# First query block of the scores: one product against both parts of the keys, the low half added through the mask

## Chip, cores and metric

The kernel runs on one core of one Trainium2 chip. The metric is the device time of one execution in microseconds (us). The kernel before was timed three times; the median is 364.83 us (364.63 to 365.72). The engines are named as the profile names them: PE is TensorE's matrix products, PEld its weight loads, DVE is VectorE, ACT is ScalarE, POOL is GpSimd, SP is SyncE, which here issues the transfers.

## What is computed

One decoder layer over 256 tokens of width 1024, all in float32. For this case the attention matters:

```python
proj = x @ w_in[l]
q, k, v = ...                       # 8 heads of 64
q = apply_partial_rope(q, cos, sin); k = apply_partial_rope(k, cos, sin)
s = einsum("hqd,htd->hqt", q, k) * scale
s = where(key_pos <= q_pos, s, -inf)
p = softmax(s, axis=-1)
y_att = einsum("hqt,htd->hqd", p, v) @ w_attn_out[l]
```

There is one block of 256 keys, so the block selection of the reference selects nothing and every query sees the keys up to its own position. Beside attention run a short gated convolution, two gates, a normalisation, and a feed-forward part of width 2816 with a second normalisation.

## The kernel before, in words

Every float32 operand of a product is split in a high part h and a low part l = x - h. A product is then made of three: h·h + h·l + l·h, summed in PSUM. For the weights ACT writes the high part (`split_h`, L196) and DVE the low part (`split_l`, L205), one unit of 128 x 1024 at a time, from a buffer `raw` that SP fills (three buffers; a transfer is issued once its buffer is free).

From the end of q, k and v on, the program goes through the units of the weights in order, `slot` by `slot` (L496). C0 is the first unit of the convolution's input h. A slot first issues the products of its unit on PE, then the ACT and PE steps that the table `beside` holds for it, then `split_h` for the unit five ahead, then `split_l` for the unit four ahead, then the DVE steps. `at` (L486) appends a step to a slot, `at_once` (L489) puts it in front of the others of its kind in that slot. Nothing else orders the work: each engine runs its instructions in the order in which they were issued, and waits at an instruction whose data or buffer isn't ready.

Two kinds of PSUM banks are used in this stage, four of each, taken in rotation. Those named acc hold the products of the units: a pair of units gets its high products by `cols_wide` (L333, 512 columns) and its low ones by `cols_narrow` (L340, 256 columns). In order of time they are h0, c0, b0, h1, c1, b1, then the gates g. So c10 and c11 (the two units of c1) take the banks of b00 and b01. A bank comes free when ACT has copied its upper half out (`conv_sum_act`, L620) and DVE has added its lower half to that (`conv_sum_dve`, L624). Those named ps hold the scores, the transposes and the results of attention.

Attention is done for four pairs of heads p = 0 to 3. `qk_transpose`, `qk_h` and `qk_l` leave in `qkT[head rows, part, group, token]` the transposed queries (groups 0 to 3) and keys (groups 4 to 7), part 0 being high and part 1 low. A pair has two heads j in the two halves of the 128 rows, so a product of the scores uses 64 rows. Then:

- `scores` (L392, product at L402) runs twice, for p = 0, 1 in slot C0+4 and for p = 2, 3 in slot C0+9. For each pair and head it has one bank: columns 0 to 127 for the first block of 128 queries (t = 0, which needs only 128 keys), columns 256 to 511 for the second (t = 1, 256 keys). Each of these is three products, and the two heads' products stand next to each other. One call is 24 products, of which 12 have 128 columns (t = 0) and 12 have 256 (t = 1).
- `masked` (L405, DVE at L412) adds the mask to the scores, scales them and finds the maximum, in one instruction per block and head, t = 0 first; L415 negates the maxima. It stands in slots C0+5, C0+7, C0+10 and C0+12.
- `exps` (L418, ACT at L423) follows one slot after each, `normalize` (L427) and `probs_T` (L435) later, then `attend`.

Of the kernel before, what the change touches and what calls it, by code (L numbers as in the profile page):

```python
# [12 lines left out]
AF = mybir.ActivationFunctionType  # L13
ALU = mybir.AluOpType

P = 128
# [11 lines left out]
SCALE = 1.0 / math.sqrt(HD)  # L28
# [109 lines left out]
def layer_kernel(ctx: ExitStack, tc: tile.TileContext, x, wpack, cpack, ln1_g, ln1_b, ln2_g, ln2_b, out):  # L138
    nc = tc.nc
# [13 lines left out]
    def ps_bank(name):  # L153
        return ps_pool.tile([P, 512], F32, tag="ps", name=name)

    def scratch(shape, name, bufs=None, tag="scr"):
        return tmp.tile(shape, F32, tag=tag, name=name, bufs=bufs or 6)
# [93 lines left out]
    MASK = [mask[:, 0:128], mask[:, 128:384]]  # L251
    PCOL = [slice(0, 128), slice(128, 384)]
# [100 lines left out]
    qkT = big.tile([P, 2, KT, S], F32R, tag="b16", name="qkT")  # L353
# [36 lines left out]
    SB, SM, PR = {}, {}, {}  # L390

    def scores(ps):  # L392

        for p in ps:
            SB[p] = [ps_bank(f"s{p}_{j}") for j in range(2)]
        for t in range(2):
            n = (t + 1) * P
            for p in ps:
                for a, b in ((0, 0), (0, 1), (1, 0)):
                    for j in range(2):  # L400
                        hs = slice(j * HD, (j + 1) * HD)
                        nc.tensor.matmul(SB[p][j][:, t * 256:t * 256 + n], qkT[hs, a, p, t * P:(t + 1) * P],  # L402
                                         qkT[hs, b, 4 + p, 0:n], start=a + b == 0, stop=a == 1)

    def masked(p):  # L405
        st = tmp.tile([P, 16], F32, tag="st", name=f"st{p}", bufs=4)
        if p == 2:
            SM["late"] = big.tile([P, 2, 2, 384], F32, tag="rows", name="sm23")
        sm = scratch([P, 2, 384], f"sm{p}", tag="pr", bufs=2) if p < 2 else SM["late"][:, p - 2]
        for t in range(2):  # L410
            for j in range(2):
                nc.vector.tensor_tensor_reduce(  # L412
                    out=sm[:, j, PCOL[t]], in0=SB[p][j][:, t * 256:t * 256 + P * (t + 1)], in1=MASK[t], scale=SCALE,
                    scalar=-3.0e38, op0=ALU.add, op1=ALU.max, accum_out=st[:, 2 * t + j:2 * t + j + 1])
        nc.vector.tensor_scalar(st[:, 4:8], st[:, 0:4], -1.0, None, op0=ALU.mult)  # L415
        SM[p] = (sm, st)
# [69 lines left out]
    def at(u, part, f, *a):  # L486
        beside.setdefault(u, {}).setdefault(part, []).append((f, a))

    def at_once(u, part, f, *a):  # L489

        beside.setdefault(u, {}).setdefault(part, []).insert(0, (f, a))
# [36 lines left out]
    C0 = U[(OFF_H, 0)]  # L528
    for t in range(2):
        at(C0 + t, "dve", rope, t)  # L530
    for g2 in (0, 2, 1, 3):
        at(C0 + 2, "pe", qk_transpose, g2)
        at(C0 + 3, "act", qk_h, g2)
        at(C0 + 3, "dve", qk_l, g2)

    at(C0 + 4, "pe", scores, (0, 1))
    at(C0 + 9, "pe", scores, (2, 3))
    for p, (m, e, n, tr, av) in enumerate(((5, 6, 8, 11, 14), (7, 8, 14, 15, 18), (10, 11, 17, 19, 22), (12, 13, 19, 21, 24))):
        at(C0 + m, "dve", masked, p)
        at(C0 + e, "act", exps, p)  # L540
        at(C0 + n, "dve", normalize, p)
        at(C0 + tr, "pe", probs_T, p)
        for j in range(2):
            at(C0 + tr + 1 + j, "act", probs_h, p, j)
            at(C0 + tr + 1 + j, "dve", probs_l, p, j)
        at(C0 + av, "pe", attend, p)
        at(C0 + av + 1, "act", attend_out, p)
        at(C0 + av + 2, "dve", attend_sum, p)
        at(C0 + av + (4 if p == 0 else 3), "act", attend_h, p)
        at(C0 + av + (4 if p < 2 else 3), "dve", attend_l, p)  # L550
# [562 lines left out]
```

## Time and profile before

| What | Value |
|---|---|
| median of three runs | 364.83 us (364.63 to 365.72) |
| the profiled execution, its own time | 365.12 us |
| its span in the trace | 363.3 us, so 1.8 us lie around it |
| busy PE, PEld | 355.9 us, 308.5 us |
| busy DVE, ACT, POOL | 298.5 us, 234.7 us, 22.5 us |
| products of the scores, L402 | 48, in two groups that begin at 52.9 and 69.6 us |

A row of the time line has the start in us from the span's start, the length in us, the engine, the line of the kernel, the operation, the tile written and the tiles read, the shape, and how many such instructions were merged; in brackets stands how long the engine had been idle before and what ended that. A product's length in the time line holds its way through the array, so products that follow each other overlap there; their rate is read from the starts. The chain that ended last is given in pieces: start, length, engine, tile, line and count.

### The profile page before, as it was taken

The page shows a single profiled execution, that of the slowest core. Times are in us where ns is not written, and L with a number is a line of the kernel's source. Part 1 is how long each engine was busy: PE and PEld are TensorE (multiplying, and loading weights), DVE is VectorE, ACT ScalarE, POOL GpSimd, SP SyncE. Part 2 cuts the span into 40 slices and gives each one's busy share as a digit, 9 for nine tenths or more (in the row PEclk, how much of TensorE's full clock was granted, in tenths as well). Part 3 has the DMA queues.
Part 4 walks back from the last instruction along what each step waited for, and adds up shares of the span by engine and source line. Part 5 has one row for each costly group of instructions (what it writes and reads, how often), then busy time and mean ns, then how long its engine had stood idle before and what let it go on. Part 6 is the DMA issues. An engine that isn't in the chain of part 4 may idle for free.

```text
span 363.3 us, 5272 instructions
## 1 busy us (share of the span) xinstructions
PE 355.9 (98%) x1955; PEld 308.5 (85%) x1955; DVE 298.5 (82%) x518; ACT 234.7 (65%) x423; POOL 22.5 (6%) x44
## 2 busy tenths in 40 slices
PE   9999999999999999999999999999999999999992
PEld 8888888889898888888888888888888888888882
DVE  4786888779795979989769798978778697999795
ACT  4675777577977966653457567666756476688901
POOL 2000000000000113301100000000000000000150
PEclk9999999999999999999999999999999999999998
DMA  8979464435654453788160835447190826663011
GB/s 284 327 290 356 161 224 182 156 115 204 261 191 146 136 224 124 241 329 290 59 233 20 326 131 220 166 180 291 58 348 19 327 81 267 233 232 115 3 58 58
DMA packets 11097, 69.62 MB, mean 192 GB/s; under 512 B 1216, under 2 KB 1472, under 8 KB 4032
## 3 DMA queue, kind: packets, MB, share of 16 engines
q1 hardware_dynamic: 10352, 67.00, 49.8%
q0 software_dynamic: 576, 2.10, 1.8%
q8 instruction: 15, 0.25, 0.3%
q10 hardware_dynamic: 144, 0.20, 0.1%
q14 instruction: 10, 0.08, 0.1%
HBM read 68.24 MB, written 1.05 MB: 191 GB/s over the span
## 4 chain that ended last, share of the span: by engine, by line
PE 95%; issue 2%; DVE 1%; POOL 1%; POOLq 0%; DVEq 0%
PE pb L333 20%; PE pb L340 11%; PE g L333 8%; PE d L315 4%; PE d L316 4%; PE d L317 4%; PE g L340 4%; PE y L333 4%; PE q L578 3%; PE k L578 3%; PE v L578 3%; PE b L333 2%; PE y L340 2%; PE c L333 2%; PE o L315 2%; PE h L333 2%
## 5 line engine op out<-in xcount | busy, mean ns | idle before, releaser
L205 DVE TENSOR_TENSOR wl<-raw,wh 128x1024 fp32r<-128x1024 f32 x99 | 121.2, 1226 | 23.8 <-ACT wh L196 23.1
L196 ACT ACTIVATE wh<-raw 128x1024 fp32r<-128x1024 f32 x99 | 103.6, 1053 | 29.3 <-DMA raw<-in_wpack 29.2
L333 PE MATMUL pb<-x1T,wh 128*128 128x512 f32 x320 | 76.2, 390 | 0.0
L333 PEld LDWEIGHTS pb<-x1T,wh 128*128 128x128 f32 x320 | 59.7, 188 | 12.1
L340 PEld LDWEIGHTS pb<-x1T,wl 128*128 128x128 f32 x320 | 41.0, 191 | 1.6
L340 PE MATMUL pb<-x1T,wl 128*128 128x256 f32 x320 | 41.5, 283 | 0.0
L228 DVE TENSOR_TENSOR wl<-raw,wh 128x1024 fp32r<-128x1024 f32 (+1 forms) x29 | 27.3, 983 | 7.3 <-ACT wh L227 7.1
L333 PE MATMUL g<-xT,wh 128*128 128x512 f32 x128 | 31.8, 395 | 0.0
L315 PE MATMUL d<-wh,f 128*128 128x512 f32 x80 | 31.4, 392 | 0.0
L316 PE MATMUL d<-wl,f 128*128 128x512 f32 x80 | 31.4, 392 | 0.0
L317 PE MATMUL d<-wh,f 128*128 128x512 f32 x80 | 31.2, 390 | 0.0
L227 ACT ACTIVATE wh<-raw 128x1024 fp32r<-128x1024 f32 (+1 forms) x29 | 23.7, 859 | 8.2 <-DMA raw<-in_wpack 4.2
L333 PEld LDWEIGHTS g<-xT,wh 128*128 128x128 f32 x128 | 23.2, 188 | 4.6
L863 DVE SCALAR_TENSOR_TENSOR fc<-fb,consts,fc 128x254 f32<-128x254 f32 x40 | 19.3, 483 | 1.4
L855 ACT ACTIVATE fc<-fb,consts 128x256 f32<-128x256 f32 x40 | 18.0, 498 | 1.9 <-DVE fb L849 1.9
L845 ACT ACTIVATE fb<-pb 128x512 f32<-128x512 f32 x20 | 11.8, 591 | 11.4 <-PE pb L340 11.4
L861 DVE SCALAR_TENSOR_TENSOR fc<-fb,consts,fc 128x255 f32<-128x255 f32 x40 | 19.1, 478 | 0.0
L317 PEld LDWEIGHTS d<-wh,f 128*128 128x128 f32 x80 | 15.0, 188 | 3.2
L315 PEld LDWEIGHTS d<-wh,f 128*128 128x128 f32 x80 | 15.1, 189 | 2.7
L316 PEld LDWEIGHTS d<-wl,f 128*128 128x128 f32 x80 | 15.1, 189 | 2.6
L340 PEld LDWEIGHTS g<-xT,wl 128*128 128x128 f32 x128 | 16.4, 191 | 0.7
L340 PE MATMUL g<-xT,wl 128*128 128x256 f32 x128 | 16.6, 283 | 0.0
(204 smaller groups left out, 600.7 us busy)
## 6 DMA issues: line engine op xcount, KB each, us to landing
raw<-in_wpack SPq DMA_DIRECT2D x55, 1024.0 KB, 4.9
raw<-in_wpack SPq DMA_DIRECT2D x6, 896.0 KB, 5.9
xr<-in_x SPq DMA_DIRECT2D x1, 1024.0 KB, 7.0
ln<-in_ln_g POOLq DMA_DIRECT2D x2, 512.0 KB, 5.5
ln<-in_ln_b POOLq DMA_DIRECT2D x2, 512.0 KB, 6.1
raw<-in_wpack SPq DMA_DIRECT2D x2, 384.0 KB, 4.1
raw<-in_wpack SPq DMA_DIRECT2D x2, 256.0 KB, 4.0
raw<-in_wpack SPq DMA_DIRECT2D x1, 512.0 KB, 5.9
```

The lines of the kernel that those rows point to most:

```text
L196: nc.scalar.activation(units[u]["h"], raw_of(u), AF.Copy)
L205: nc.vector.tensor_tensor(units[u]["l"], raw_of(u), units[u]["h"].bitcast(F32), op=ALU.subtract)
L227: nc.scalar.activation(h, src, AF.Copy)
L228: (eng or nc.vector).tensor_tensor(l, src, h.bitcast(F32), op=ALU.subtract)
L315: nc.tensor.matmul(o, ah, bh, start=start, stop=False)
L316: nc.tensor.matmul(o, ah, bl, start=False, stop=False)
L317: nc.tensor.matmul(o, al, bh, start=False, stop=stop)
L333: nc.tensor.matmul(bank, un["h"][:, k, n0:n0 + P], b[:, k].rearrange("p a s -> p (a s)"), start=k == 0, stop=False)
L340: nc.tensor.matmul(bank[:, 0:S], un["l"][:, k, n0:n0 + P], b[:, k, 0], start=False, stop=k == nk - 1)
L578: nc.tensor.matmul(banks[m][t], (xl if p == 2 else xh)[:, k, t * P:(t + 1) * P], wl if p == 1 else wh, start=k == 0 and p == 0, stop=k == ...
L861: nc.vector.scalar_tensor_tensor(c[:, 1:S], pb[:, a * S:a * S + S - 1], w_ffn(1, j), c[:, 1:S], op0=ALU.mult, op1=ALU.add)
L863: nc.vector.scalar_tensor_tensor(c[:, 2:S], pb[:, a * S:a * S + S - 2], w_ffn(0, j), c[:, 2:S], op0=ALU.mult, op1=ALU.add)
```

## The change

For t = 0 the three products of a head become two. The first has the queries' high part as weights and both parts of the keys, 2 x 128 columns, as the moving operand; it writes 256 columns of the bank, which before held nothing in columns 128 to 255. The second is l·h as before, on columns 0 to 127. A new step `masks_low` copies columns 128 to 255 of both heads to a tile `lo` with ACT, and POOL adds the mask to it. `masked` then takes t = 1 first, and for t = 0 it uses `lo` in place of the mask.

`masks_low` stands in front of the other ACT steps of slots C0+5 (p = 0), C0+6 (p = 1), C0+10 (p = 2) and C0+11 (p = 3).

```diff
-                for a, b in ((0, 0), (0, 1), (1, 0)):
+                for a, b in ((0, slice(0, 2)), (1, 0)) if t == 0 else ((0, 0), (0, 1), (1, 0)):
                     for j in range(2):
                         hs = slice(j * HD, (j + 1) * HD)
-                        nc.tensor.matmul(SB[p][j][:, t * 256:t * 256 + n], qkT[hs, a, p, t * P:(t + 1) * P],
-                                         qkT[hs, b, 4 + p, 0:n], start=a + b == 0, stop=a == 1)
+                        o = SB[p][j][:, t * 256:t * 256 + n]
+                        if t == 0 and a == 0:
+                            o = SB[p][j][:, 0:256].rearrange("p (a n) -> p a n", a=2)
+                        nc.tensor.matmul(o, qkT[hs, a, p, t * P:(t + 1) * P], qkT[hs, b, 4 + p, 0:n],
+                                         start=a == 0 and b != 1, stop=a == 1)
+
+    def masks_low(p):
+
+        SM["lo", p] = scratch([P, 2, P], f"lo{p}", tag="fc", bufs=4)
+        for j in range(2):
+            nc.scalar.activation(SM["lo", p][:, j], SB[p][j][:, 128:256], AF.Copy)
+        nc.gpsimd.tensor_tensor(SM["lo", p], SM["lo", p], MASK[0][:, None, :].to_broadcast([P, 2, P]), op=ALU.add)
...
-        for t in range(2):
+        for t in (1, 0):
             for j in range(2):
                 nc.vector.tensor_tensor_reduce(
-                    out=sm[:, j, PCOL[t]], in0=SB[p][j][:, t * 256:t * 256 + P * (t + 1)], in1=MASK[t], scale=SCALE,
+                    out=sm[:, j, PCOL[t]], in0=SB[p][j][:, t * 256:t * 256 + P * (t + 1)],
+                    in1=MASK[1] if t else SM["lo", p][:, j], scale=SCALE,
...
+        at_once(C0 + m - p % 2, "act", masks_low, p)
         at(C0 + m, "dve", masked, p)
```

## Prediction

> **What bounds the kernel now.** The page comes first: the engines' shares and the chain that ended last.
>
> ```profile
> PE 355.9 (98%) x1955; PEld 308.5 (85%) x1955; DVE 298.5 (82%) x518; ACT 234.7 (65%) x423; POOL 22.5 (6%) x44
> ...
> PE 95%; issue 2%; DVE 1%; POOL 1%; POOLq 0%; DVEq 0%
> ```
>
> PE is busy 98% of the span and carries 95% of the chain. A busy PE in this view need not run at its best, so I ask who made PE wait, over the whole span:
>
> ```profile
> engine line waited for: us in total, times, longest us
> PE warm L241 <- PEq L1103: 0.8, 1, 0.8
> ```
>
> One wait, before the first product. No transfer, no weight and no bank holds PE up afterwards. So work taken off PE is worth its full length, as long as the change brings no wait. The stretches in which the change acts:
>
> ```profile
> 50.00:60.00 10.00, 10.00 (x74) 8.61 (x73) 7.71 (x19) 8.11 (x17) 0.00 (x0) 1.00 0.44 167
> 60.00:70.00 10.00, 10.00 (x66) 8.88 (x64) 8.81 (x25) 6.52 (x17) 0.00 (x0) 1.00 0.58 209
> 70.00:80.00 10.00, 10.00 (x71) 8.74 (x68) 7.13 (x25) 5.42 (x16) 0.00 (x0) 1.00 0.31 107
> ```
>
> The columns are PE, PEld, DVE, ACT, POOL, then the granted clock and the share of the transfers. PE is full at a clock of 1.00, ACT has 2 to 4.5 us free in each ten, DVE 1.2 to 2.9, POOL does nothing.
>
> **What the change takes off PE.** The chain in order of time (start, length, what) gives the rates:
>
> ```profile
> 52.98 1.59 PE s L402 x24
> ...
> 64.09 3.65 PE c L333 x16
> 67.74 1.91 PE c L340 x16
> 69.65 1.57 PE s L402 x24
> ...
> 77.03 0.11 PE ptp L439
> ...
> 85.34 0.12 PE av L458
> ```
>
> A product of 512 columns costs 3.65 / 16 = 0.228 us, one of 256 columns 1.91 / 16 = 0.119, one of 128 columns 0.11. Halving 256 columns saves almost nothing: every product pays about 0.11, which I read as the load of its weights. The 24 products of a call run as 12 pairs, the two heads together. Their starts, from narrow windows of the time line (each row begins with the earliest product still running):
>
> ```profile
> 53.19 0.39 PE L402 MATMUL s<-qkT 64*128 64x128 f32 x4
> ...
> 53.52 0.45 PE L402 MATMUL s<-qkT 64*128 64x128 f32 x4
> ...
> 53.63 0.57 PE L402 MATMUL s<-qkT 64*128 64x256 f32 x6
> ...
> 53.93 0.40 PE L402 MATMUL s<-qkT 64*128 64x256 f32 x4
> ...
> 54.16 0.41 PE L402 MATMUL s<-qkT 64*128 64x256 f32 x4
> ```
>
> Pairs three to six of 128 columns: (53.52 - 53.19) / 3 = 0.11 each. Pairs three to five of 256 columns: (54.16 - 53.93) / 2 = 0.115; I take the longer 0.119 of the chain. For t = 0 a call has six pairs now, 6 x 0.11 = 0.66 us. After the change it has two pairs of 256 and two of 128 columns: 2 x 0.119 + 2 x 0.11 = 0.46. That is 0.20 us a call and **0.40 us** for the two calls.
>
> Bounds: if the wider pairs cost no more than narrow ones, two pairs of 0.11 go in each call, 0.44 in all. At the other end stands the step from narrow to wide: from 53.63 to 53.93 the first two wide pairs take 0.30, so the first takes about 0.18. If each wide pair among narrow ones cost that, a call would save 0.66 - 0.58 = 0.08, 0.16 in all. I keep 0.119, because that row is a run of its own kind, while the 0.18 is the change of pace paid once, and t = 1 still pays it. That two stretches of 128 columns cost more than one of 256 is excluded by the last chain row: L458 reads and writes just such a form at 0.12.
>
> The Trainium skill, in TensorE: Matmul & The Clock Gate, Back-to-back issue gap, gives an isolated product N / 2.4 + 2.5 ns, time that goes with the columns. By it the change saves 3 ns a pair of heads, since 384 columns stream either way. The rows of 0.11 and 0.119 speak against it; the page itself adds that loads of weights set the spacing too.
>
> **What it adds, and where.** Eight ACT copies, four POOL additions, and a wait of DVE for POOL. The rows of ACT and DVE around both calls:
>
> ```profile
> 54.24 0.29 DVE L412 CUSTOM_DVE_ANT_0 sm<-s,mask 128x128 f32<-128x128 f32 x1 [1.43 <-PE s L402]
> ...
> 55.48 0.17 DVE L415 TENSOR_SCALAR st<-st 128x4 f32<-128x4 f32 x1
> 55.55 0.42 DVE L624 TENSOR_TENSOR cc<-c,cc 128x256 f32<-128x256 f32 x1
> 55.68 0.40 ACT L423 ACTIVATE sm<-sm,st 128x128 f32<-128x128 f32 x1 [1.60 <-DVE st L415]
> ...
> 57.60 0.38 ACT L620 ACTIVATE cb<-b 128x256 f32<-128x256 f32 x1
> 57.88 1.05 ACT L196 ACTIVATE wh<-raw 128x1024 fp32r<-128x1024 f32 x1
> ...
> 58.97 1.23 DVE L205 TENSOR_TENSOR wl<-raw,wh 128x1024 fp32r<-128x1024 f32 x1 [0.52 <-ACT wh L196]
> ...
> 61.41 0.42 DVE L624 TENSOR_TENSOR cb<-b,cb 128x256 f32<-128x256 f32 x1
> ...
> 63.92 3.82 PE L333 MATMUL c<-xT,wh 128*128 128x512 f32 x16
> ...
> 65.58 1.05 ACT L196 ACTIVATE wh<-raw 128x1024 fp32r<-128x1024 f32 x1
> ...
> 70.90 0.29 DVE L412 CUSTOM_DVE_ANT_0 sm<-s,mask 128x128 f32<-128x128 f32 x1 [1.72 <-PE s L402]
> ...
> 77.39 0.49 ACT L445 ACTIVATE vpt<-ptp 128x384 fp32r<-128x384 f32 x1 [1.97 <-PE ptp L441]
> ```
>
> No row shows a copy of 128 x 128 out of PSUM. The nearest is L620 at twice the columns: 0.38 long, the next instruction 0.28 later. I price the copies at that, too dear rather than too cheap.
>
> POOL and one conflict with it:
>
> ```profile
> L468 POOL TENSOR_TENSOR ac<-ac x4: 739/748/986, 87.1 to 121.0; 128x256 f32<-128x256 f32 x4
> ...
> 57.03 0.68 DVE L629 TENSOR_TENSOR z<-cc,ch 128x512 f32<-128x512 f32 x1
> ...
> 87.13 0.76 POOL L468 TENSOR_TENSOR ac<-ac 128x256 f32<-128x256 f32 x1 [84.51 <-ACT ac L467]
> ...
> 87.54 0.89 DVE L629 TENSOR_TENSOR z<-cc,ch 128x512 f32<-128x512 f32 x1
> ```
>
> An addition of this size takes 0.75 us (0.74 to 0.99). Beside it DVE's L629 took 0.89 instead of 0.68. The Trainium skill (SBUF — State Buffer, Who interferes with whom) says that a DVE instruction with two SBUF inputs and a POOL one that reads SBUF shut each other out; the two rows agree. Here that can hold a low half of DVE for at most one addition, 0.75.
>
> *First call.* The scores of p = 0, which released DVE at 54.24, come 0.20 earlier, 54.04. ACT copies at 54.04 and 54.32, done at 54.70; POOL adds until 55.5. DVE reduces t = 1 meanwhile, then t = 0 (two of 0.21 and what follows): L415 at about 56.05 instead of 55.48, L624 0.55 late. ACT has behind the copies what used to be done before them: the copy of c01 (0.28), the high half of unit C0+10 (0.95 to the next), the copies of p = 1 (0.56 and their end), then the table load of 1.28 that stands before the first `exps`. So: 54.60, 54.88, 55.83, 56.49, and `exps` of p = 0 at 57.8 instead of 55.68. It is **2.1 us late**, set by ACT's own queue; the maxima are ready 1.5 us earlier, so POOL's addition could take three times as long unseen. Everything behind on ACT is as late: the copy of b00 (57.60), the high half (57.88), so DVE's low half (58.97), `masked` of p = 1 behind it, and the sum that frees b01's bank: 61.41 + 0.42 = 61.83 becomes about 63.95. POOL blocking DVE vanishes in DVE's wait for that high half.
>
> The first to want something of this is PE: c11 takes b01's bank at the middle of the 16 products from 63.92, 63.92 + 8 x 0.228 - 0.20 = 65.54. It was free 3.9 us ahead and will be 1.6 us ahead. The weights split late here are for units C0+10 and later, which PE meets after the second call at 69.6. **No wait of PE.**
>
> *Second call.* ACT, 2.1 late (65.58 becomes 67.7, its unit done at 68.8), now waits itself for the scores of p = 2, which released DVE at 70.90 and come 0.40 earlier, 70.50. There the lateness ends. Copies, addition and reductions put `exps` of p = 2 some 0.5 late again, but ACT idled 1.97 us before 77.39, and so meets probs_T with over a us to spare. From there all follows PE, 0.40 us earlier.
>
> Sum: the profiled execution took 365.12 us (span 363.3 and 1.8 around it); it becomes 365.12 - 0.40 = 364.72. It lies 0.29 above the median of the runs shown, 364.83, from which I forecast 364.83 - 0.40 = **364.43 us**.
>
> **The rivals.**
>
> 1. *Time goes with columns*, as in the rule above, or a wide pair among narrow ones costs 0.18. Gain 0.01 to 0.16, so 364.67 to 364.82. For it: the step at 53.63. Against it: 0.11 for 128 and 0.119 for 256 columns in four places. Chance 0.17.
> 2. *Slower: c11 waits for b01's bank.* Place: PE at 65.5, behind the chain ACT copies, exps, b01's copy, DVE's sum. It decides from a lateness of 3.7 us at that sum; I get 2.1. Four copies and the table load stand in it, so copies at 0.68 instead of 0.28 to the next would just reach it. If each cost 1.2 us, lateness is 2.1 + 4 x 0.92 = 5.8, PE loses 2.1, and the time is 364.43 + 2.1 = 366.5. For it: ACT is the busiest in 50 to 60 (8.11 of 10). Against it: no ACT copy of this kind comes near; the 1.2 is beyond the 1.05 of 1024 columns. Chance 0.07.
> 3. *It doesn't shorten the end*: PE's 0.40 is lost later to something now hidden, 364.83. For it: nothing but that the tail holds DVE and POOL work (5% of the chain). Against it: that tail is released by PE. Chance 0.05.
>
> **How the numbers follow.** Forecast 0.68, rivals 0.17, 0.07 and 0.05; 0.03 for a gain that nothing here explains. The gain's bounds 0.16 and 0.44 put the median at 364.39 to 364.67. The runs shown scatter from 0.20 below to 0.89 above their median, and a new median can do part of it: I go twice 0.20 down, to 364.0, and from the no-gain case 364.83 half of 0.89 up, to 365.2. Rival 2 is left out above. A measurement of this kernel tells about 0.3% (1.1 us) from no change. Faster by more: 0.03. Within: 0.91. Slower by more: 0.06, rival 2 where it goes past 365.9.
>
> **What would show it.** Right: each call's piece in the chain falls from 1.59 and 1.57 to about 1.38; no new wait of PE; `exps` of p = 0 about 2 us late; ACT idle before the second copies with PE's scores as releaser; the row at 77.39 0.4 earlier. Wrong: a wait of PE at c or b with DVE's L624 of after as releaser; pieces of over 1.5 us; POOL additions of over 2 us; a lateness that is still there at the gates.

## The result, and the profile after

| | runs | median | range | ratio to before, 95% interval |
|---|---|---|---|---|
| before | 12 | 364.93 us | 363.97 to 365.72 | |
| after | 12 | 364.31 us | 363.64 to 365.15 | 0.998 (0.9971 to 0.9988) |
| after, measured again beside 29 runs of before (364.89) | 12 | 363.94 us | 363.59 to 365.05 | 0.9978 (0.9966 to 0.9989) |

The change gains 0.62 us by the medians, 0.73 us by the ratio (0.44 to 1.06). The forecast was 364.43 and a gain of 0.40: the time is 0.12 off and in the range, but the two intervals of the gain begin at 0.44 and at 0.40, so it is probably larger than 0.40. Where the rest comes from is the question of the experiments.

The page of the changed kernel, the waits of PE, and its chain in order of time:

```profile
span 362.8 us, 5271 instructions
...
PE 355.3 (98%) x1947; PEld 307.0 (85%) x1947; DVE 299.9 (83%) x518; ACT 235.4 (65%) x431; POOL 24.9 (7%) x48
```

```profile
engine line waited for: us in total, times, longest us
PE warm L241 <- PEq L1116: 0.8, 1, 0.8
PE v L591 <- ACT wh L227: 0.3, 1, 0.3
```

```profile
53.25 1.36 PE s L406 x20
...
69.68 1.37 PE s L406 x19
```

ACT has eight instructions more (431 for 423), POOL four (48 for 44). PE's second wait is at v, in the first ten us, where the first weights arrive; in the stage of the change there is none. The score groups fall from 1.59 and 1.57 to 1.36 and 1.37 (x19 for 20: one record is missing from the trace).

The time line of the first call. In this execution the scores begin at 53.18, which is 0.27 later than in the trace of before, because the first weights came later:

```profile
53.18 1.43 PE L406 MATMUL s<-qkT 64*128 64x256 f32 x20
...
54.29 0.45 ACT L413 ACTIVATE lo<-s 128x128 f32<-128x128 f32 x2 [2.47 <-PE s L406]
...
54.88 1.07 ACT L196 ACTIVATE wh<-raw 128x1024 fp32r<-128x1024 f32 x1
54.89 0.75 POOL L414 TENSOR_TENSOR lo<-lo,mask 128x256 f32<-128x256 f32 x1 [52.27 <-ACT lo L413]
...
55.67 0.29 DVE L423 CUSTOM_DVE_ANT_0 sm<-s,lo 128x128 f32<-128x128 f32 x1 [0.29 <-POOL lo L414]
...
56.22 0.17 DVE L427 TENSOR_SCALAR st<-st 128x4 f32<-128x4 f32 x1
...
56.31 1.28 ACT L435 ACT_TABLE_LOAD   x1
56.37 0.74 POOL L414 TENSOR_TENSOR lo<-lo,mask 128x256 f32<-128x256 f32 x1 [0.73 <-ACT lo L413]
...
56.63 1.56 DVE L205 TENSOR_TENSOR wl<-raw,wh 128x1024 fp32r<-128x1024 f32 x1
57.60 0.40 ACT L435 ACTIVATE sm<-sm,st 128x128 f32<-128x128 f32 x1
...
63.16 0.42 DVE L637 TENSOR_TENSOR cb<-b,cb 128x256 f32<-128x256 f32 x1
...
63.95 3.82 PE L333 MATMUL c<-xT,wh 128*128 128x512 f32 x16
```

ACT copies both halves in 0.45, POOL adds in 0.75, DVE waits only 0.29 for POOL. The maxima are negated at 56.22, the table load ends at 57.59, `exps` begins at 57.60: ACT's own queue sets it, as forecast. DVE's low half at 56.63 takes 1.56 instead of 1.22; it runs beside POOL's second addition (56.37 to 57.11). In e10 below the same low half begins at 56.42, after that addition has ended (56.15), and takes 1.21. The sum that frees b01's bank ends at 63.58; the ninth product of c1 begins at 63.95 + 8 x 0.228 = 65.77. The margin is **2.2 us**.

The starts of the single pairs, again from narrow windows, each row beginning with the earliest product still running:

```profile
53.40 0.39 PE L406 MATMUL s<-qkT 64*128 64x128 f32 x4
...
53.46 0.56 PE L406 MATMUL s<-qkT 64*128 64x256 f32 x6
...
53.63 0.40 PE L406 MATMUL s<-qkT 64*128 64x128 f32 x4
...
53.68 0.46 PE L406 MATMUL s<-qkT 64*128 64x256 f32 x4
...
53.86 0.40 PE L406 MATMUL s<-qkT 64*128 64x256 f32 x4
```

The pairs for t = 0 are wide at 53.18, narrow at 53.40, wide at 53.46 and narrow at 53.63; t = 1 begins at 53.68. From a wide pair to the narrow one behind it pass 0.17 us (0.22 for the first pair of the group, whose step was 0.16 before, where a narrow pair stood first), from a narrow pair to the wide one behind it only 0.06. One of each takes 0.23 (53.40 to 53.63). The traces of e0 and e10 and the second call have the same steps.

The second call, and where the lateness ends:

```profile
70.72 0.45 ACT L413 ACTIVATE lo<-s 128x128 f32<-128x128 f32 x2 [2.33 <-PE s L406]
...
72.77 0.40 ACT L435 ACTIVATE sm<-sm,st 128x128 f32<-128x128 f32 x1
...
77.22 0.49 ACT L457 ACTIVATE vpt<-ptp 128x384 fp32r<-128x384 f32 x1 [1.37 <-PE ptp L453]
```

ACT waits 2.33 us for the scores, so nothing of the first call's lateness is left, and 1.37 us again before probs_T.

**Where the time went.** Two stretches of each trace tell it: from the first product of h0 (38.10 before, 38.37 after) to the start of the last product, and from there to the span's end. First the time line of before, then that of after:

```profile
38.10 3.79 PE L333 MATMUL h<-xT,wh 128*128 128x512 f32 x16
...
356.38 0.28 PE L317 MATMUL e<-wh,f 128*128 128x256 f32 x1
```

```profile
38.37 3.79 PE L333 MATMUL h<-xT,wh 128*128 128x512 f32 x16
...
356.21 0.28 PE L317 MATMUL e<-wh,f 128*128 128x256 f32 x1
```

The first stretch falls from 318.28 to 317.84, by 0.44: that is the two score groups (0.23 + 0.20). The second falls from 6.96 to 6.60 us. These **0.36 us** after the last product were in no term of the forecast. They lie in POOL's closing steps; the rows of its last line in the final 2 us, before and after:

```profile
L1109 POOLq DRAIN  x2: 40/71/102, 362.4 to 363.1; - x2
L1109 POOLq EVENT_SEMAPHORE_RANGE_CLEAR  x1: 139/139/139, 362.9 to 362.9; - x1
```

```profile
L1122 POOLq DRAIN  x2: 40/71/102, 362.2 to 362.5; - x2
L1122 POOLq EVENT_SEMAPHORE_RANGE_CLEAR  x1: 139/139/139, 362.4 to 362.4; - x1
```

Each row gives the first and last start. Before, POOL's drain starts at 362.4 and the clearing of semaphores 0.5 later; after, 0.13 later (by the trace's starts). The last steps of all engines follow that clearing.

### The profile page after: what moved, and what is told of

The parts are those of the page before. It is cut to its first block, busy times and chain, and to the rows that moved or that the text cites. A ratio compares the mean times of both kernels' runs of the same rounds, so it can differ in the third digit from the quotient of the medians.

```text
span 362.8 us, 5271 instructions
## 1 busy us (share of the span) xinstructions
PE 355.3 (98%) x1947; PEld 307.0 (85%) x1947; DVE 299.9 (83%) x518; ACT 235.4 (65%) x431; POOL 24.9 (7%) x48
## 4 chain that ended last, share of the span: by engine, by line
PE 92%; issue 2%; DMA 2%; DVE 1%; POOL 1%; SPq 0%; ACT 0%; POOLq 0%; DVEq 0%
PE pb L333 20%; PE pb L340 11%; PE g L333 8%; PE d L315 4%; PE d L316 4%; PE d L317 4%; PE g L340 4%; PE y L333 4%; PE q L591 3%; PE v L591 3%; PE k L591 3%; PE b L333 2%; PE y L340 2%; PE c L333 2%; PE h L333 2%; PE o L316 2%
## 5 line engine op out<-in xcount | busy, mean ns | idle before, releaser
L1024 POOL TENSOR_TENSOR fs<-fs 128x512 f32<-128x512 f32 (+2 forms) x5 | 5.8, 1163 | 169.7 <-ACT fs L1021 169.5
```

## The experiments

The theories: A, only PE's shorter groups count (0.43 us); B, the moved steps of ACT and DVE bring something too; C, the rest is scatter. Later D, the number of POOL's instructions decides the 0.36 us at the end, against E, something in the added steps. Each kernel's two stretches, from the starts in its trace:

| kernel | POOL instructions | POOL records in all | h0 to last product | last product to end |
|---|---|---|---|---|
| before | 44 | 72 | 318.28 | 6.96 |
| after | 48 | 77 | 317.84 | 6.60 |
| e0, after again | 48 | 77 | 317.83 | 6.59 |
| e1, wide products only | 44 | 72 | 317.85 | 6.95 |
| e2, steps only | 48 | 77 | 318.30 | 6.60 |
| e3, high products only | 44 | 72 | 316.46 | 6.93 |
| e4, before and 4 on POOL | 48 | 76 | 318.30 | 6.59 |
| e5, after and 4 off POOL | 44 | 73 | 318.29 | 7.09 |
| e6, ACT later by one copy | 48 | 77 | 317.84 | 6.59 |
| e7, by four copies | 48 | 77 | 320.04 | 6.59 |
| e8, before and 1 on POOL | 45 | 73 | 318.33 | 7.09 |
| e9, before and 2 on POOL | 46 | 74 | 318.32 | 7.00 |
| e10, t = 0 first | 48 | 77 | 317.87 | 6.60 |

The second column counts what the page counts, the third every record of POOL in the trace, its semaphore steps, drains and transfer issues included.

### e0: the changed kernel again

No edit.

> The changed kernel once more, beside the kernel before on the same chip. Theory A (only PE's shorter score groups count, all added work is hidden): the chain pieces of the scores stay near 1.37 us against 1.59 and 1.57, and the time falls by 0.43 us, ratio 0.9988. Theory B (the moved steps of ACT and DVE bring something beside PE's time): the fall is again 0.6 to 0.7 us, ratio 0.998. Theory C (the difference between 0.43 and the first measurement is the scatter of the start and the end): the ratio's interval takes in 0.9988.

Measured: 0.9978 (0.9966 to 0.9989), 363.94 against 364.89. The interval takes in A's 0.9988, which is what C asked for, so the times alone do not exclude C. Against C stands the trace: the end is 6.59 again, where the kernel before has 6.96. The gain is 0.80 us by the ratio.

### e1: the wide products without the steps

```diff
-        at_once(C0 + m - p % 2, "act", masks_low, p)
-        for t in (1, 0):
+        for t in range(2):
-                    in1=MASK[1] if t else SM["lo", p][:, j], scale=SCALE,
+                    in1=MASK[t], scale=SCALE,
```

> The wide products alone: the added half of the bank is never read, so the product of the queries' high part with the keys' low part is left out for the first query block; masked is as before. Theory A: the same as the whole change, 0.43 us under before, since ACT's, POOL's and DVE's part of the change cost nothing; exps of p = 0 stands where it stood before less 0.2. Theory B: 0.2 to 0.3 us slower than the whole change. If the added steps cost something that PE's trace does not show: faster than the whole change.

Measured: 0.9986 (0.9974 to 0.9998), 364.51. PE's stretch is that of the whole change, 317.85, with score pieces of 1.36 and 1.37. So the added steps cost PE nothing. But the end is 6.95, as before. The median lies 0.57 over that of e0; the two intervals overlap, so it is the end, 6.95 against 6.59, that shows something of the steps, which A called free, to be worth time.

### e2: the steps without the wide products

```diff
-                for a, b in ((0, slice(0, 2)), (1, 0)) if t == 0 else ((0, 0), (0, 1), (1, 0)):
+                for a, b in ((0, 0), (0, 1), (1, 0)):
...
-            nc.scalar.activation(SM["lo", p][:, j], SB[p][j][:, 128:256], AF.Copy)
+            nc.scalar.activation(SM["lo", p][:, j], SB[p][j][:, 0:128], AF.Copy, scale=0.0)
```

> The steps alone: the scores' products are those of before, and ACT copies the first half of the bank with a factor of 0, so that the tile holds the mask after POOL's addition; order and waits are those of the change. Theory A: no change against before (ratio 1.000), exps of p = 0 about 2 us late, PE with no wait and score pieces of 1.59 and 1.57. Theory B: 0.2 to 0.3 us faster than before. Rival 2 of the prediction (lateness reaches a bank): slower, with a wait of PE.

Measured: 0.9992 (0.9979 to 1.0004), 364.62; PE's stretch 318.30 as before, no wait, score pieces 1.59 and 1.57, `exps` of p = 0 at 57.57. The time alone doesn't tell A from B. The trace does: the end is 6.60. The steps bring 0.36 us at a place where none of them stands, 290 us later.

### e3: how much a product is worth

```diff
-                for a, b in ((0, 0), (0, 1), (1, 0)):
+                for a, b in ((0, 0),):
```

(with `start=True, stop=True`.)

> The kernel before with only the product of the two high parts in the scores, for both blocks (two of three products left out): eight of twelve pairs of a call go, 4 x 0.11 + 4 x 0.119 = 0.92 us, 1.83 us for the two calls. Theory A: the time falls by 1.8 us, ratio 0.995. If PE's time in this stage does not reach the end (rival 3): no change. If the time goes with the columns: 4 x 0.056 + 4 x 0.109 = 0.66 a call, 1.3 us.

Measured: 0.9945 (0.9926 to 0.9963), 362.98, which is 1.9 us less; PE's stretch 318.28 - 316.46 = 1.82. Sixteen pairs are worth 1.83 us at 0.11 and 0.119, and 1.37 if time went with the columns at the 0.228 us of 512 columns. The sum doesn't go with the columns here, and what PE saves reaches the end whole. The Trainium skill, in TensorE: Matmul & The Clock Gate, Back-to-back issue gap, gives for an isolated product a time that goes with the columns, and says that in a stream the loads of weights count too; the 1.82 speaks against the first. That the loads are the reason was not tried by itself.

### e4 and e5: four POOL instructions

```diff
     for i, f in enumerate(INV_FREQ):
         nc.gpsimd.memset(invf[:, i:i + 1], f)
+    spare = cst.tile([P, 4], F32, name="spare")
+    for i in range(4):
+        nc.gpsimd.memset(spare[:, i:i + 1], 0.0)
```

> The kernel before with four more POOL instructions (fills of a spare tile of 4 columns) near its start, where POOL is idle; nothing reads them. In the traces so far the stretch from the last product's start to the span's end is 6.96, 6.95 and 6.93 us in the kernels with 44 POOL instructions and 6.60, 6.59 and 6.60 in those with 48. Theory D (the number of POOL instructions decides it: the last of them, the clearing of semaphores, waits for a late fetch of instructions when there are 44): 6.60 here, score pieces as before, time 0.36 us less, ratio 0.9990. Theory E (it is something in the added steps themselves, such as ACT's or DVE's order): 6.95 and no change of the time.

Measured: 0.9987 (0.9979 to 0.9996), 364.46; the end 6.59, PE's stretch 318.30. Four fills that nobody reads, 360 us ahead of the end, shorten the kernel. D's number holds and E falls; why it counts is the question of e8 and e9.

In e5 the changed kernel gives four of the eight fills to DVE:

```diff
     for i, f in enumerate(INV_FREQ):
-        nc.gpsimd.memset(invf[:, i:i + 1], f)
+        (nc.gpsimd if i < 4 else nc.vector).memset(invf[:, i:i + 1], f)
```

> The changed kernel with four of POOL's eight fills of the table of frequencies given to DVE, so that POOL has 44 instructions again. Theory D: the stretch after the last product goes back to 6.95, and only PE's 0.43 us are left, ratio 0.9988. Theory E: 6.60 and the ratio of the whole change, 0.998.

Measured: 0.9991 (0.998 to 1.0002), 364.79. The end goes back, to 7.09 rather than 6.95. The count of all records tells why: POOL has 73 here and not the 72 of before, because the first addition of `masks_low` brings a semaphore step of its own. e8 below has 73 too, and the same 7.09. PE's stretch, 318.29, was not expected; PE's waits in e5:

```profile
PE qkt L378 <- DVE qk L370: 0.2, 1, 0.2
```

In this execution h0 began early, at 37.63, and from there to the scores PE took 15.26 us instead of 14.81: it stood at the transposes until DVE's rotation of q and k was done. An early start alone doesn't do it: e10's h0 began at 37.40, and its scores 14.81 later. That DVE's four fills made the wait is likely, but was not tried by itself.

### e6 and e7: how far the steps may be late

```diff
+        for _ in range(N if p == 1 else 0):        # N = 1 in e6, 4 in e7
+            nc.scalar.activation(qk[:, 0], qk[:, 0], AF.Copy)
         nc.gpsimd.tensor_tensor(SM["lo", p], SM["lo", p], MASK[0][:, None, :].to_broadcast([P, 2, P]), op=ALU.add)
```

> The changed kernel with one useless ACT copy of 128 x 1024 (about 1.1 us) behind the copies of p = 1, ahead of exps of p = 0; its result is not used. In the changed kernel the sum that frees the bank of b01 ends at 63.58 and the ninth product of c1 begins at 65.77: a margin of 2.2 us. My reading: the lateness grows to 3 us, the margin shrinks to 1.1, no wait of PE, the time is that of the changed kernel within 0.2 us. If the margin is smaller than I read it, PE waits at c for DVE's sum.

Measured: 0.9983 (0.9974 to 0.9992), 364.25; PE's stretch 317.84, no new wait. A us more of lateness costs nothing.

> The same with four such copies, one behind the other, 4.3 to 4.6 us. My reading: the margin of 2.2 us is used up and PE waits 2.1 to 2.4 us at the ninth product of c1 with DVE's sum as its releaser; the time is 2.1 to 2.4 us over that of the changed kernel, ratio to before 1.004. If the order of the ACT steps has no such limit here (a lateness that never reaches PE): no change. If another bank or the weights stand in front: the wait is at another product, or longer.

Measured: 1.0037 (1.0024 to 1.0051), 366.36; PE's stretch 320.04, which is 2.20 more. The time line of e7, ACT and PE:

```profile
55.89 4.37 ACT L415 ACTIVATE qk<-qk 128x1024 f32<-128x1024 f32 x4
```

```profile
64.21 2.12 PE L333 MATMUL c<-xT,wh 128*128 128x512 f32 x8 [0.37 <-DVE cb L639]
67.60 2.11 PE L333 MATMUL c<-xT,wh 128*128 128x512 f32 x8 [1.27 <-DVE cb L639]
```

4.37 us of copies less the margin of 2.2 make the 2.2 that PE loses, at the products of c, released by DVE's sums. (The idle times in brackets are smaller than the loss because the modelled ends of the products reach into the pause.) What was not expected: a first, short wait stands already at c10, for the bank of b00. Rival 2 of the prediction is real, at its place; it begins 2.2 us beyond the change.

### e8 and e9: where POOL pauses

As e4, with one and two fills.

> The kernel before with one more POOL instruction (a fill of a spare tile that nothing reads). In the kernel before, the pause of POOL in the closing sequence stands ahead of the clearing of semaphores (0.50 us from the start of the drain ahead of it to its own, against 0.13 in the changed kernel). If the pause belongs to a place in POOL's stream of instructions: one more instruction ahead moves it one closing instruction forward, to the drain, and the stretch after the last product stays near 7.0. If the number of instructions has nothing to do with it: as in the kernel before.

> The same with two more POOL instructions. If the pause belongs to a place in the stream: it moves two closing instructions forward, to POOL's semaphore steps, still near 7.0, or it vanishes under the wait for the output transfers and the stretch is 6.6. If not: as in the kernel before.

One run each, so the traces count, not the times (364.62 and 365.35 beside 364.87). The closing rows of e8, then of e9:

```profile
L1112 POOLq EVENT_SEMAPHORE  x4: 17/17/17, 361.6 to 362.7; - x4
L1112 POOLq DRAIN  x2: 40/137/234, 362.1 to 362.6; - x2
L1112 POOLq EVENT_SEMAPHORE_RANGE_CLEAR  x1: 139/139/139, 362.4 to 362.4; - x1
```

```profile
L1112 POOLq EVENT_SEMAPHORE  x4: 17/17/17, 362.4 to 363.5; - x4
L1112 POOLq DRAIN  x2: 40/94/148, 363.0 to 363.3; - x2
L1112 POOLq EVENT_SEMAPHORE_RANGE_CLEAR  x1: 139/139/139, 363.1 to 363.1; - x1
```

By the starts counted from the last product, the first two semaphore steps, the drain and the clearing stand at 5.86, 5.94, 6.02, 6.52 before; at 5.86, 5.93, 6.38, 6.64 in e8; at 5.86, 6.29, 6.38, 6.56 in e9; at 5.86, 5.94, 6.03, 6.16 after. The step that pauses begins 0.35 to 0.37 us later behind the one ahead of it than the same step does in after, and the pause moves one closing instruction forward with each instruction added, as it must if it belongs to a place in the stream. Counted over all of POOL's records, the step that pauses is the 69th in before, e1, e3, e5, e8 and e9 alike. In e5 it is the drain, as in e8, and begins at 6.38 as there. With four fills more the 69th place has left the closing steps and 6.6 is left.

Where the pause went, the transfers of the instruction queue tell (in the view of the DMA queues: queue, kind, packets, MB, share of the stretch). The first row is before from 362.9 to 364.5 us, the second e4 from 178 to 180:

```profile
q14 instruction: 1, 0.01, 1.7%
...
q14 instruction: 1, 0.01, 1.5%
```

It is one packet of 8 KB, at 363.6 in before and at 178.7 in e4. The other way round there is none: before has no packet from 178 to 180, e4 none from 362 to 364. The other packets of this queue after 30 us stand at the same places in both kernels within 1 us, so four fills on POOL moved this one packet. At 178.7 POOL is in an idle time of 169 us, in which a pause costs nothing. All six traces with the pause have such a packet behind the last product, 0.7 us after the start of the step that paused; the seven without the pause have none there. So the pause goes with a fetch of instructions, but POOL does not wait for this packet: it has gone on 0.7 us before the packet begins.

### e10: the old order of masked

```diff
-        for t in (1, 0):
+        for t in range(2):
```

> The changed kernel with masked in the old order, t = 0 first, so that DVE waits for POOL's addition with nothing to do meanwhile. My reading: for p = 0 the negated maxima come about 0.6 us later than in the changed kernel, exps of p = 0 stays bound by ACT's own queue (the table load ends 1.2 us after the maxima), PE has no new wait, the score pieces and the stretch after the last product are those of the changed kernel. If the order matters to the time: a wait of PE at c or b.

One run: 363.64 beside 364.87. PE's only new wait is 0.4 us at q, in the first five us; its stretch is 317.87, end 6.60, score pieces 1.36 and 1.37. The maxima come at 55.94 with scores that began at 52.21, 3.73 us behind them instead of 3.04 (56.22 and 53.18), 0.7 later; `exps` follows 4.43 behind them instead of 4.42. The order is worth nothing here: ACT's queue covers it.

## Why the prediction was right, and where its size was not

- **What bounds.** Right: PE has no wait in the stage before, after, or in e1, and PE's time reaches the end one to one (e3, 1.82 of 1.83).
- **The sum on PE.** 0.20 a call forecast, 0.23 and 0.20 measured, 0.44 by the stretch, the forecast's upper bound. The total was right and its two prices were not. The sum took 0.119 for a wide pair and 0.11 for a narrow one; by the starts the steps are 0.17 and 0.06, together the same 0.23. So the 0.18 that the lower bound set for a wide pair among narrow ones did come, and what the bound had wrong is the narrow pair behind it, which takes half of 0.11. No row of before has such a mixture, and that the two errors cancel was luck.
- **The lateness.** `exps` of p = 0 was put 4.9 us behind the first score (57.8 and 52.91), and came 4.42 behind it. Before it came 2.77 behind it (55.68), so it is 1.65 late and not 2.1. Most of the difference is the copies, priced rather too dear: two took 0.45 and not 0.66. The margin at c11 was 2.2 and not 1.6, and e7 confirms it. POOL's addition cost DVE's low half 0.34 at 56.63 (1.56 for 1.22), under the bound of 0.75; it was hidden, for DVE stood idle 0.97 us before its next sum at 59.77, with ACT as releaser. The row of probs_T on ACT, 77.39, came at 77.22: 0.44 earlier once the 0.27 of the later start are taken off.
- **The step that failed: the sum.** "From there all follows PE, 0.40 us earlier" stopped at the last product. The closing sequence was taken as fixed, and it lost 0.36 us of its own; that term of the sum was missing, not mis-sized. 0.44 + 0.36 = 0.80 is what both traces show and lies within both intervals. e4 shows that the four POOL instructions alone give it, in a kernel in which nothing else of the change is present.
- **The rivals.** 1 (columns) falls with e1 and e3. 2 (a bank that comes late) is right in place and mechanism, and begins, by the margin and by what e7 lost, at 2.2 us more lateness than the change has. 3 (lost before the end) falls with e3.
- What stays open is what POOL does in the 0.36 us at that place of its stream. A fetch of instructions goes with the pause (e8, e9), but the packet seen begins only after it, and no view here shows POOL waiting for one.

## What to carry to other kernels

A product need not be cheaper because it is narrower: here 128 columns took 0.11 us and 256 took 0.119, though 512 took 0.228. Compare the starts of a narrow and a wide stream in the same trace, and where they come at nearly the same pace, try to join two narrow products that share their weights. Read the gain from the whole group: in a mixture the single steps differ (0.17 and 0.06) from those of a stream of one kind. Work put on other engines is free only up to the margin at the next bank that they free; add it up along the slowest queue, then read the margin from the sum's end to the product that takes the bank. When a gain of a few tenths of a us does not fit the sum, split the span at the last product before looking for a cause in the edit.

## What was not expected of the hardware

The number of instructions on an engine that is 93% idle moved the end of the kernel by 0.36 us (6.96 with 72 records of POOL, 6.60 with 77), in steps that could be followed instruction by instruction (e8, e9): a pause stands at the 69th record, and in these kernels it costs time only where that record is one of the closing steps. A measured gain of this size can come from an edit's instruction count alone, and a kernel with four useless fills on POOL (e4) was faster than the one without, by 0.13% (0.04 to 0.21).
